# A one-layer NSA trunk: last output piece stored in two, a bias table written in longer runs, bias loads placed later

## The chip, the cores and the metric

One core of a Trainium2 chip runs the whole program. The metric is device time in microseconds of one execution. Shown are the median of three runs and one profiled execution, which the trace below belongs to.

## The reference, cut to what matters

One layer of native sparse attention on 512 tokens of width 1024, in float32, between two RMS norms:

```
u = rms_norm(x, pre_gain)
q, k/v (six sets), gates, z = u @ w_in
kc, vc = compress_kv(...)                 # a small two-layer net on blocks of 32 tokens
logits += table[t5_bucket(distance)]      # one bias table for all three branches
o = softmax branches (compressed, selected, window)
y = sum(gates * o * silu(z)) @ w_out
out = x + rms_norm(y, post_gain)
```

The bias depends only on the distance and the head. The kernel therefore makes two tables of it early on: `toepd`, 16 heads by 640 distances, for the window and selected branches, and `cmpb`, 1024 distances by 16 heads, for the compressed branch.

## The kernel before

All products run as three passes of split float32 (a high and a low part of each operand). Weights come in tiles of 512 KB (`load_raw`, L100, three buffers `wr`) and are split by `split_raw` (L106) into `wh` and `wl` (three buffers each): even tiles by ACT and POOL, odd ones by DVE alone (L240). SyncE (SP) issues nearly every transfer, in one queue, so an issue that waits holds up what is behind it. A scheduler lays out the order of each engine's instructions from the program text; the text's order is what the author controls.

**The head (0 to about 110 us).** `rms` and `prep` (L304, L311) make the normed, transposed input `uh`, `ul`. Then come the projection for compressed keys (`p_kc`, L367 to L377) and, between its two halves, `tables()` (L330). `tables()` multiplies a constant one-hot matrix by the bias table. For `cmpb` it does so in eight column blocks `j`: the 33x128 slice of `hcr` is loaded as weights and the 33x16 table `nth`, then `ntl`, streams through (L351, L352). The result, `cb`, has the distances on its 128 partitions, eight blocks of 16 heads each. Four stores (L356) bring it to DRAM, one for each group `g` of four heads:

```
for g in range(G):
    SP.dma_start(dview(cmpb, g * H * MC * R, [[R, 128], [128 * R, 8], [1, R]]), cb[:, g])
load_bias(0)
```

Partition `m` and block `j` hold distance `j*128 + m`, so each run in DRAM is R = 4 floats, 16 bytes, and a store has 1024 of them. `load_bias(0)` (L160) then loads four `bias` tiles from `toepd` (L163) and the compressed-branch bias `cbs` from `cmpb` (L168). `blocks` (L402) copies the projected keys, then values, out of PSUM in blocks (`blk`, L407, on DVE) and splits them (`bh` on ACT, L416; `bl` on DVE and POOL, L417). The loop at L472 projects `p_v` for both other value sets and runs the first layer of the compression net (`mlp`, L420); it reads tiles 4 to 11 of the weight order (tile 6 is the first one that SP asks for behind the bias loads).

**The tail.** `wout` (L820) multiplies by `w_out`, row tile by row tile in the order 0, 3, 2, 1. For the last one, each half of 512 columns is multiplied by the post gain into `g3` (L915); ACT sums its squares (L912); POOL makes the norm factor `ss` (`rstd`, L84). `finish` (L873) then does `xr = g3 * ss + xr` on DVE (L874) and stores the half from SP (L877):

```
for i in range(2):
    finish(*prev, i)
```

Of the kernel before, what the change touches and what calls it, by code (L numbers as in the profile page):

```python
# [14 lines left out]
ALU = mybir.AluOpType  # L15
# [4 lines left out]
S = 512  # L20
D = 1024
H = 16
DH = 64
G = 4
R = 4
# [9 lines left out]
MC = 64  # L35
# [11 lines left out]
def dview(ap, off, dims):  # L47
    return bass.AP(tensor=ap.tensor, offset=ap.offset + off, ap=dims)
# [3 lines left out]
def nsa_layer(ctx: ExitStack, tc: tile.TileContext, x, pre_gain, post_gain, table, w_in, w_out,  # L52
              k_pos, k_w1, k_w2, v_pos, v_w1, v_w2, hot, hot_c, out):
    nc = tc.nc
    V, A, P, T, SP = nc.vector, nc.scalar, nc.gpsimd, nc.tensor, nc.sync
    x = x.rearrange("b s d -> (b s) d")
    out = out.rearrange("b s d -> (b s) d")
# [102 lines left out]
    def load_bias(g):  # L160
        for hh in range(R):
            b = keep.tile([128, S], F32, name="bias", tag="bias", bufs=6)
            SP.dma_start(b, dview(toepd, (g * R + hh) * LT, [[1, 128], [1, S]]))  # L163
            bias[g * R + hh] = b
        c = keep.tile([128, NT, CP, R], F32, name="cbs", tag="cbs", bufs=1)
        for t in range(NT):
            src = dview(cmpb, (g * H * MC + 8 * t) * R, [[R, 8], [MC * R, 16], [1, CP * R]])
            SP.dma_start(c[:, t].rearrange("p c r -> p (c r)"), src)  # L168
        cbs[g] = c
# [90 lines left out]
    with tc.tile_pool(name="a1", bufs=1) as a1:  # L260
        grow = a1.tile([1, D], F32, name="grow")
        A.dma_start(grow, pre_gain)
        warm = a1.tile([1, 1], F32, name="warm")
        A.activation(warm, nhalf[0:1], AF.Tanh)
        one = a1.tile([1, 128], F32, name="one")
        V.memset(one, 1.0)
        ones = a1.tile([1, 128], F32R, name="ones")
        V.tensor_copy(ones, one)
        xs = []
        for t in range(NT):  # L270
            xt = a1.tile([128, D], F32, name="xt", bufs=4)
            SP.dma_start(xt, x[t * 128:(t + 1) * 128, :])
            xs.append(xt)
            if t == 1:
                load_ahead(1)
        tabx = a1.tile([33, H], F32, name="tabx")
        SP.dma_start(tabx[0:32], table)
        hots = a1.tile([33, LT], F32, name="hots")
        SP.dma_start(hots, hot)
        hotc = a1.tile([33, D], F32, name="hotc")  # L280
        SP.dma_start(hotc, hot_c)
        for nm, pos, w2 in (("k", k_pos, k_w2), ("v", v_pos, v_w2)):
            small[nm, "p"] = sm.tile([32, 2, DH], F32, name="pos" + nm)
            SP.dma_start(small[nm, "p"][:, 0], pos.rearrange("n l d -> (n l) d"))
            small[nm, "w"] = sm.tile([128, 2, DH], F32, name="w2" + nm)
            SP.dma_start(small[nm, "w"], w2.rearrange("n (k p) c -> p (n k) c", p=128))
        gain = []
        gh = a1.tile([1, D], F32R, name="gh")
        gl = a1.tile([1, D], F32R, name="gl")
        for i in range(2):  # L290
            hs = slice(i * 512, (i + 1) * 512)
            V.tensor_copy(gh[:, hs], grow[:, hs])
            V.tensor_tensor(gl[:, hs], grow[:, hs], gh[:, hs].bitcast(F32), op=ALU.subtract)
            p = sb()
            T.matmul(p, ones, gh[:, hs], start=True, stop=False)
            T.matmul(p, ones, gl[:, hs], start=False, stop=True)
            gain.append(p)
        sq = a1.tile([128, D], F32, name="sq")
        banks = [tb, ob, tb]
        nb_ = 0  # L300

        rs_ = {}

        def rms(t):  # L304
            ss = a1.tile([128, 1], F32, name="ss", bufs=4)
            tc.keep_in_program_order(A.activation(sq, xs[t], AF.Square, scale=1.0 / 32, accum_out=ss))
            r = a1.tile([128, 1], F32, name="r", bufs=4)
            rstd(r, ss)
            rs_[t] = r

        def prep(t):  # L311
            nonlocal nb_
            r = rs_[t]
            for kq in range(2):
                hs = slice(kq * 512, (kq + 1) * 512)
                V.scalar_tensor_tensor(xs[t][:, hs], xs[t][:, hs], r, gain[kq], op0=ALU.mult, op1=ALU.mult)
                p = banks[nb_ % 3]()
                nb_ += 1
                for j in range(4):
                    k = kq * 4 + j  # L320
                    T.transpose(p[:, j * 128:(j + 1) * 128], xs[t][:, k * 128:(k + 1) * 128], ident)
                for jj in range(2):
                    i = kq * 2 + jj
                    src = p[:, jj * 256:(jj + 1) * 256].rearrange("p (a b) -> p a b", a=2)
                    dh = uh[i][:, :, t * 128:(t + 1) * 128]
                    dl = ul[i][:, :, t * 128:(t + 1) * 128]
                    A.copy(dh, src)
                    V.tensor_tensor(dl, src, dh.bitcast(F32), op=ALU.subtract)

        def tables():  # L330
            ntab = a1.tile([33, H], F32, name="ntab")
            V.tensor_scalar(ntab[0:32], tabx[0:32], -1.0, None, op0=ALU.mult)
            V.memset(ntab[32:33], BIG)
            nth = a1.tile([33, H], F32R, name="nth")
            ntl = a1.tile([33, H], F32R, name="ntl")
            V.tensor_copy(nth, ntab)
            V.tensor_tensor(ntl, ntab, nth.bitcast(F32), op=ALU.subtract)
            hsr = a1.tile([33, LT], F32R, name="hsr")
            hcr = a1.tile([33, D], F32R, name="hcr")
            A.copy(hsr, hots)  # L340
            A.copy(hcr, hotc)
            for o, n in ((0, 512), (512, LT - 512)):
                p = sb()
                T.matmul(p[:H, :n], nth, hsr[:, o:o + n], start=True, stop=False)
                T.matmul(p[:H, :n], ntl, hsr[:, o:o + n], start=False, stop=True)
                V.tensor_copy(toep[:, o:o + n], p[:H, :n])
            SP.dma_start(toepd, toep)
            cb = sm.tile([128, G, 8, R], F32, name="cb")
            p = sb()
            for j in range(8):  # L350
                T.matmul(p[:, j * H:(j + 1) * H], hcr[:, j * 128:(j + 1) * 128], nth, start=True, stop=False)  # L351
                T.matmul(p[:, j * H:(j + 1) * H], hcr[:, j * 128:(j + 1) * 128], ntl, start=False, stop=True)  # L352
            V.tensor_copy(cb.rearrange("p g j r -> p j g r"),
                          p[:, :8 * H].rearrange("p (j g r) -> p j g r", g=G, r=R))
            for g in range(G):
                SP.dma_start(dview(cmpb, g * H * MC * R, [[R, 128], [128 * R, 8], [1, R]]), cb[:, g])  # L356
            load_bias(0)

        rms(0)
        rms(1)  # L360
        prep(0)
        split_ahead(0)
        prep(1)
        split_ahead(1)
        rms(2)
        rms(3)
        p_kc = [pj(), pj()]  # L367
        for hh in range(2):
            hs = slice(hh * 256, (hh + 1) * 256)
            for k in range(KT):  # L370
                if hh == 0 and k in (3, 5):
                    prep(2 if k == 3 else 3)
                h, l = tiles[k // 4]
                for m in range(2):
                    ms = slice(m * 128, m * 128 + 128)
                    pass3(p_kc[m][:, hs], h[:, k % 4, ms], l[:, k % 4, ms], uh[k // 2][:, k % 2, hs],
                          ul[k // 2][:, k % 2, hs], k == 0, k == KT - 1)  # L377
            if hh == 0:
                tables()

    with tc.tile_pool(name="a2", bufs=1) as a2:
# [90 lines left out]
        for kp in range(4):  # L472
            h, l = tile_(n)
            for kk in range(2):
                k = kp * 2 + kk
                a, b = (v.rearrange("p (k a) c -> p k (a c)", k=2)[:, kk] for v in (h, l))
                for t in range(NT):
                    ts = slice(t * 128, (t + 1) * 128)
                    sh, sl = uh[k // 2][:, k % 2, ts], ul[k // 2][:, k % 2, ts]
                    T.matmul(p_v[t], sh, a, start=k == 0, stop=False)  # L480
                    T.matmul(p_v[t], sl, a, start=False, stop=False)
                    T.matmul(p_v[t], sh, b, start=False, stop=k == KT - 1)
            mlp(n + 1, kp, p_mk, kb)
            n += 2
        hs = silu2(p_mk)
        for t in range(NT):
            src = p_v[t].rearrange("p (i g d) -> p i g d", i=2, g=G)
# [10 lines left out]
        p = tb()  # L498
# [321 lines left out]
    def wout():  # L820
# [49 lines left out]
        def last(i):  # L870
            return tc.keep_in_program_order(i)
# [8 lines left out]
        for j, t in enumerate(turn):  # L880
# [43 lines left out]
                    for i in range(2):  # L924
                        finish(*prev, i)
            prev = t, xr, ss
        for i in range(2):
            finish(*prev, i)

    def kproj(g0):  # L930
        alloc_kd(g0)
# [95 lines left out]
```

## Time and profile before

| | |
|---|---|
| median of three runs | 466.47 us (466.29 to 467.47) |
| the profiled execution's own time | 466.85 us |
| its span, first to last instruction | 465.0 us |
| mean granted TensorE clock | 0.993 |
| PE busy | 450.9 us, 97% of the span |
| DVE, ACT, POOL busy | 330.6, 274.3, 184.7 us |
| share of PE in the chain that ended last | 89% |

The profiled execution lies 0.38 us above the median of the runs, and its time is 1.85 us longer than its span. PE is TensorE's matrix work and PEld its weight loads; the idle time of the other engines matters only where PE waits for one of them.

### The profile page before, as it was taken

The page shows a single profiled execution, that of the slowest core. Times are in us where ns is not written, and L with a number is a line of the kernel's source. Part 1 is how long each engine was busy: PE and PEld are TensorE (multiplying, and loading weights), DVE is VectorE, ACT ScalarE, POOL GpSimd, SP SyncE. Part 2 cuts the span into 40 slices and gives each one's busy share as a digit, 9 for nine tenths or more (in the row PEclk, how much of TensorE's full clock was granted, in tenths as well). Part 3 has the DMA queues.
Part 4 walks back from the last instruction along what each step waited for, and adds up shares of the span by engine and source line. Part 5 has one row for each costly group of instructions (what it writes and reads, how often), then busy time and mean ns, then how long its engine had stood idle before and what let it go on. Part 6 is the DMA issues. An engine that isn't in the chain of part 4 may idle for free.

```text
span 465.0 us, 6924 instructions
## 1 busy us (share of the span) xinstructions
PE 450.9 (97%) x2330; PEld 375.3 (81%) x2330; DVE 330.6 (71%) x801; ACT 274.3 (59%) x642; POOL 184.7 (40%) x185
## 2 busy tenths in 40 slices
PE   5999999999999999999999999999999999999994
PEld 4797888878888878888888788888878888888883
DVE  6869844851766888768769776885896667567685
ACT  5712232542766577767846867666776666467541
POOL 4424544242223453342463525245343342448212
PEclk9989999999999999999999999999999999999998
DMA  8489275263111321511132332024051211214113
GB/s 300 142 82 280 77 216 162 66 206 90 47 45 48 112 59 34 182 45 47 45 90 70 88 94 71 21 57 132 19 180 45 92 45 47 91 43 140 47 45 135
DMA packets 45501, 44.63 MB, mean 96 GB/s; under 512 B 7751, under 2 KB 38471, under 8 KB 45466
## 3 DMA queue, kind: packets, MB, share of 16 engines
q1 hardware_dynamic: 44424, 44.00, 31.9%
q8 instruction: 18, 0.29, 0.3%
q10 hardware_dynamic: 1042, 0.20, 0.2%
q14 instruction: 17, 0.14, 0.1%
HBM read 41.99 MB, written 2.20 MB: 95 GB/s over the span
## 4 chain that ended last, share of the span: by engine, by line
PE 89%; DVE 4%; ACT 3%; issue 2%; POOL 1%; DVEq 0%; POOLq 0%; ACTq 0%
PE ps_pj L146 11%; PE ps_pj L148 11%; PE ps_pj L147 11%; PE ps_s L591 9%; PE ps_t L681 7%; PE ps_o L715 4%; PE ps_o L714 4%; PE ps_pj L834 3%; PE ps_pj L835 3%; PE ps_pj L836 3%; PE ps_s L247 2%; PE ps_s L248 2%; PE ps_s L249 2%; PE ps_pj L247 2%; PE ps_pj L248 1%
## 5 line engine op out<-in xcount | busy, mean ns | idle before, releaser
L118 POOL TENSOR_TENSOR wl<-wr,wh 128x512 fp32r<-128x512 f32 x94 | 123.0, 1328 | 138.6 <-ACT wh L113 122.2
L146 PE MATMUL ps_pj<-uh,wh 128*128 128x512 f32 x240 | 99.0, 412 | 0.0
L148 PE MATMUL ps_pj<-ul,wh 128*128 128x512 f32 x240 | 94.2, 393 | 0.0
L147 PE MATMUL ps_pj<-uh,wl 128*128 128x512 f32 x240 | 94.2, 392 | 0.0
L604 ACT ACTIVATE p<-p,nm 128x512 f32<-128x512 f32 (+3 forms) x128 | 71.6, 560 | 24.3 <-DVE nm L603 23.5
L685 DVE TENSOR_TENSOR ptl<-ps_t,pth 128x512 fp32r<-128x512 f32 x80 | 55.0, 688 | 28.2 <-ACT pth L684 27.7
L113 ACT CAST wh<-wr 128x1024 fp32r<-128x1024 f32 x47 | 49.2, 1047 | 43.5 <-DMA wr<-in_nsa_w_in_dram 20.1
L591 PE MATMUL ps_s<-kd,q 128*128 128x512 f32 (+5 forms) x256 | 63.9, 336 | 0.7 <-DVE zs L699 0.6
L684 ACT CAST pth<-ps_t 128x512 fp32r<-128x512 f32 x80 | 46.4, 580 | 29.3 <-PE ps_t L681 28.7
L148 PEld LDWEIGHTS ps_pj<-ul,wh 128*128 128x128 f32 x240 | 45.1, 188 | 10.1
L591 PEld LDWEIGHTS ps_s<-kd,q 128*128 128x128 f32 x256 | 43.9, 189 | 9.0 <-DVE zs L699 1.2
L146 PEld LDWEIGHTS ps_pj<-uh,wh 128*128 128x128 f32 x240 | 45.2, 188 | 6.1
L147 PEld LDWEIGHTS ps_pj<-uh,wl 128*128 128x128 f32 x240 | 45.3, 189 | 5.8
L603 DVE CUSTOM_DVE_ANT_0 p<-ps_s,bias 128x128 f32<-128x128 f32 (+3 forms) x80 | 34.6, 447 | 20.7 <-PE ps_s L591 20.5
L681 PE MATMUL ps_t<-ident,p 128*128 128x128 f32 x320 | 48.4, 272 | 0.0
L681 PEld LDWEIGHTS ps_t<-ident,p 128*128 128x128 f32 x320 | 39.7, 140 | 9.4
L714 PE MATMUL ps_o<-pth,vt 128*128 128x512 f32 x80 | 33.7, 421 | 0.0
L603 DVE CUSTOM_DVE_ANT_1 p<-ps_s,bias 128x256 f32<-128x256 f32 (+2 forms) x48 | 26.3, 555 | 9.3 <-PE ps_s L591 8.6
L728 POOL TENSOR_TENSOR y<-otmp,zs 128x256 f32<-128x256 f32 x16 | 12.3, 771 | 51.5 <-DVE otmp L725 51.5
L715 PE MATMUL ps_o<-ptl,vt 128*128 128x512 f32 x80 | 32.3, 404 | 0.0
L730 POOL TENSOR_TENSOR otmp<-otmp,zs 128x256 f32<-128x256 f32 x15 | 11.1, 741 | 37.9 <-DVE otmp L725 37.9
L569 ACT ACTIVATE zs<-ps_pj 128x512 f32<-128x512 f32 x22 | 13.1, 596 | 19.4 <-PE ps_pj L148 19.3
(268 smaller groups left out, 895.6 us busy)
## 6 DMA issues: line engine op xcount, KB each, us to landing
wr<-in_nsa_w_in_dram SPq DMA_DIRECT2D x36, 512.0 KB
wr<-in_nsa_w_in_dram SPq DMA_DIRECT2D x16, 256.0 KB
bias<-toepd SPq DMA_DIRECT2D x16, 256.0 KB
wr<-in_nsa_w_out_dram SPq DMA_DIRECT2D x8, 512.0 KB
xt<-in_x_dram SPq DMA_DIRECT2D x4, 512.0 KB
wr<-in_nsa_cmp_k_w_dram SPq DMA_DIRECT2D x4, 512.0 KB
wr<-in_nsa_cmp_v_w_dram SPq DMA_DIRECT2D x4, 512.0 KB
xr<-in_x_dram SPq DMA_DIRECT2D x8, 256.0 KB
```

Of the source, the lines that this page charges most:

```text
L113: A.copy(h[:, 0:kn], raw[:, 0:kn])
L118: el.tensor_tensor(l[:, ks], raw[:, ks], h[:, ks].bitcast(F32), op=ALU.subtract)
L146: T.matmul(p, a, rh, start=k == 0, stop=False)
L147: T.matmul(p, b, rh, start=False, stop=False)
L148: T.matmul(p, a, rl, start=False, stop=k == KT - 1)
L591: T.matmul(po, qs[h][:, qt * 128:(qt + 1) * 128], kds[h // R][:, i, c0:c0 + n], start=i == 0, stop=i == 1)
L603: V.tensor_tensor_reduce(pd, src, bi, 1.0, BIG, ALU.add, ALU.min, st["nm"][:, hh:hh + 1])
L604: A.activation(po, po, AF.Exp, bias=st["nm"][:, hh:hh + 1], scale=-1.0, accum_out=st["rs"][:, hh:hh + 1])
L681: T.transpose(tp[:, hh * 128:(hh + 1) * 128], st["p"][hh][:, c:c + 128], ident)
L685: V.tensor_tensor(pl, tp, ph.bitcast(F32), op=ALU.subtract)
L714: T.matmul(acc, v, ph, start=j == 0, stop=False)
L715: T.matmul(acc, v, pl, start=False, stop=j == qt)
```

## The change

Three edits. (1) In `tables()` the weights of block `j` are now the columns `j, j+8, j+16, ...` of `hcr` (a stride of eight floats, 32 bytes) instead of 128 neighbours. Partition `m` then holds the distances `8m` to `8m+7`, and a group's store writes one run of 8*R floats, 128 bytes, from each partition. (2) `load_bias(0)` is called after the loop at L472 and no longer inside `tables()`. (3) The last row tile's second half is finished in two pieces of 256 columns; the first is stored from ACT's queue, the second from SP's.

```diff
+            hcj = hcr.rearrange("p (m j) -> p j m", j=8)
             for j in range(8):
-                T.matmul(p[:, j * H:(j + 1) * H], hcr[:, j * 128:(j + 1) * 128], nth, start=True, stop=False)
-                T.matmul(p[:, j * H:(j + 1) * H], hcr[:, j * 128:(j + 1) * 128], ntl, start=False, stop=True)
+                T.matmul(p[:, j * H:(j + 1) * H], hcj[:, j], nth, start=True, stop=False)
+                T.matmul(p[:, j * H:(j + 1) * H], hcj[:, j], ntl, start=False, stop=True)
...
-                SP.dma_start(dview(cmpb, g * H * MC * R, [[R, 128], [128 * R, 8], [1, R]]), cb[:, g])
-            load_bias(0)
+                SP.dma_start(dview(cmpb, g * H * MC * R, [[8 * R, 128], [1, 8 * R]]),
+                             cb[:, g].rearrange("p j r -> p (j r)"))
...
             mlp(n + 1, kp, p_mk, kb)
             n += 2
+        load_bias(0)
         hs = silu2(p_mk)
...
-        for i in range(2):
-            finish(*prev, i)
+        t, xr, ss = prev
+        finish(t, xr, ss, 0)
+        for c, q_ in ((0, A), (256, SP)):
+            cs = slice(c, c + 256)
+            last(V.scalar_tensor_tensor(xr[1][:, cs], g3[1][:, cs], ss, xr[1][:, cs], op0=ALU.mult, op1=ALU.add))
+            q_.dma_start(out[t * 128:(t + 1) * 128, S + c:S + c + 256], xr[1][:, cs])
```

What the scheduler made of it: the queue of SP in the head, from the `toepd` store on (`wr` are weight tiles; line numbers of the changed kernel are a few higher).

```order
 L347 DMA toepd<-toep 16x640
-L356 DMA cmpb<-cb 128x8x4 x4
-L163 DMA bias<-toepd 128x512 x4
+L357 DMA cmpb<-cb 128x32 x4
+L163 DMA bias<-toepd 128x512
+L103 DMA wr<-in_nsa_w_in_dram 128x2x256 x2
+L163 DMA bias<-toepd 128x512
+L103 DMA wr<-in_nsa_cmp_k_w_dram 128x4x256
+L163 DMA bias<-toepd 128x512 x2
 L168 DMA cbs<-cmpb 128x1x128 x4
-L103 DMA wr<-in_nsa_w_in_dram 128x2x256 x2
-L103 DMA wr<-in_nsa_cmp_k_w_dram 128x4x256
```

The weight tiles 6 (two transfers of 128x2x256) and 7 moved ahead of three of the four bias loads and of the four `cbs` loads; one bias load still stands ahead of them.

The end of DVE's queue before:

```order
L915 TENSOR_TENSOR og_5065<-ps_pj,pgain 128x512
L874 SCALAR_TENSOR_TENSOR xr<-og_5032,fss,xr 128x512
L874 SCALAR_TENSOR_TENSOR xr<-og_5065,fss,xr 128x512
L1023 UNCONDITIONAL_BRANCH
```

and in the change:

```order
L917 TENSOR_TENSOR og_5065<-ps_pj,pgain 128x512
L876 SCALAR_TENSOR_TENSOR xr<-og_5032,fss,xr 128x512
L933 SCALAR_TENSOR_TENSOR xr<-og_5065,fss,xr 128x256 x2
L1029 UNCONDITIONAL_BRANCH
```

ACT's queue, which ended with the last sum of squares, now ends with the store of the first piece:

```order
L914 ACTIVATE junk,sumsq<-ps_pj 128x512
L934 DMA out_dram<-xr 128x256
L1029 UNCONDITIONAL_BRANCH
```

On all engines the order of everything else is the same in both kernels, line numbers aside.

## Rows read from the trace of the kernel before

**Rows 1.** What PE waited for from 20 to 95 us: total, times, longest.

```profile
PE ps_s L480 <- DVE blk L407: 0.6, 1, 0.6
PE ps_o L427 <- DVE wl L118: 0.4, 1, 0.4
```

**Rows 2.** Timeline of SP's queue in the head: start us, us until the last issue, transfer.

```profile
23.45 0.33 SPq L347 DMA_DIRECT2D toepd<-toep  x1
25.07 3.17 SPq L356 DMA_DIRECT2D cmpb<-cb  x4
28.34 2.50 SPq L163 DMA_DIRECT2D bias<-toepd  x4
30.88 5.54 SPq L168 DMA_DIRECT2D cbs<-cmpb  x4
37.63 1.03 SPq L103 DMA_DIRECT2D wr<-in_nsa_w_in_dram  x2
```

**Rows 3.** Timeline of ACT, POOL and DVE: tile 6 split, first readers of bias and `cbs`.

```profile
43.46 1.05 ACT L113 CAST wh<-wr 128x1024 fp32r<-128x1024 f32 x1 [4.65 <-DMA wr<-in_nsa_w_in_dram]
44.59 2.52 POOL L118 TENSOR_TENSOR wl<-wr,wh 128x512 fp32r<-128x512 f32 x2 [3.66 <-ACT wh L113]
...
116.20 0.69 DVE L603 CUSTOM_DVE_ANT_0 p<-ps_s,bias 128x512 f32<-128x512 f32 x1 [3.39 <-PE ps_s L591]
121.44 0.38 DVE L656 TENSOR_TENSOR lc<-ps_s,cbs 128x128 f32<-128x128 f32 x1 [0.47 <-PE ps_s L591]
```

**Rows 4.** Timeline of PE: last reader of tile 3, the wait, first reader of tile 6.

```profile
41.71 0.39 PE L249 MATMUL ps_s<-ul,wh 128*128 128x512 f32 x1
...
44.98 0.47 PE L480 MATMUL ps_s<-wh,uh 128*128 128x512 f32 x1 [0.61 <-DVE blk L407]
...
49.63 0.40 PE L480 MATMUL ps_pj<-wh,uh 128*128 128x512 f32 x1
```

**Rows 5.** Timeline of PE: first and last of the 16 small matmuls, and what follows.

```profile
22.77 0.27 PE L351 MATMUL ps_s<-nth,hcr 33*128 33x16 f32 x1
...
24.46 0.25 PE L352 MATMUL ps_s<-ntl,hcr 33*128 33x16 f32 x1
...
25.02 0.41 PE L248 MATMUL ps_pj<-uh,wl 128*128 128x256 f32 x1
...
27.80 0.41 PE L249 MATMUL ps_pj<-ul,wh 128*128 128x256 f32 x1
...
28.17 0.28 PE L248 MATMUL ps_pj<-uh,wl 128*128 128x256 f32 x1
...
30.44 0.28 PE L249 MATMUL ps_pj<-ul,wh 128*128 128x256 f32 x1
```

**Rows 6.** Busy us by stretch: PE, PEld, DVE, ACT, POOL, then PEclk, DMA share, GB/s.

```profile
24.60:28.00 3.40, 3.40 (x17) 3.38 (x17) 1.36 (x5) 0.00 (x0) 0.52 (x1) 0.51 0.91 136
```

**Rows 7.** Groups by shape, weight loads of 22 to 25 us: busy, mean ns.

```profile
L351 PEld LDWEIGHTS ps_s<-nth,hcr 33*128 33x128 f32 x8 | 1.5, 187 | 0.1
```

**Rows 8.** Groups by shape, DVE from 110 to 145 us: 128 columns, strided and not.

```profile
L603 DVE CUSTOM_DVE_ANT_0 p<-ps_s,bias 128x128 f32<-128x128 f32 x2 | 0.5, 284 | 0.0
...
L656 DVE TENSOR_TENSOR lc<-ps_s,cbs 128x128 f32<-128x128 f32 x1 | 0.4, 380 | 0.5 <-PE ps_s L591 0.5
```

**Rows 9.** Timeline of DVE: a split beside a busy POOL, and one beside an idle POOL.

```profile
38.09 1.73 DVE L417 TENSOR_TENSOR bl<-blk,bh 128x496 fp32r<-128x496 f32 x1
...
41.38 0.68 DVE L118 TENSOR_TENSOR wl<-wr,wh 128x512 fp32r<-128x512 f32 x1
```

**Rows 10.** Timeline of the end: DVE's last two instructions and SP's last two stores.

```profile
460.72 1.42 DVE L874 SCALAR_TENSOR_TENSOR xr<-og,fss,xr 128x512 f32<-128x512 f32 x2 [0.35 <-POOL fss L90]
461.50 0.33 SPq L877 DMA_DIRECT2D out_dram<-xr  x1
462.16 0.33 SPq L877 DMA_DIRECT2D out_dram<-xr  x1
```

**Rows 11.** Groups by shape, DVE from 440 to 466 us: 512 and 256 columns.

```profile
L907 DVE TENSOR_TENSOR og<-og,ps_pj 128x512 f32<-128x512 f32 x3 | 2.1, 688 | 1.2 <-PE ps_pj L836 1.2
...
L731 DVE TENSOR_TENSOR y<-y,otmp 128x256 f32<-128x256 f32 x1 | 0.4, 419 | 0.0
```

**Rows 12.** Stretches as in rows 6: the first bias and `cbs` transfers, the last stores.

```profile
30.00:36.00 6.00, 6.00 (x30) 4.94 (x30) 5.06 (x11) 1.05 (x1) 2.55 (x2) 1.00 0.88 34
...
462.30:463.70 1.40, 0.00 (x0) 0.00 (x0) 0.00 (x0) 0.00 (x0) 0.00 (x0) 0.50 0.98 369
```

## The prediction, made before the changed kernel ran

> **What bounds the kernel now.** The page comes first: PE is busy for 97% of the span and makes up 89% of the chain that ended last. An edit therefore pays only where PE waits, where PE itself works longer, or after PE's last matmul. Next, the list of what PE waited for, cut to the stretch that the edits touch (20 to 95 us). It holds two waits, 0.61 and about 0.4 us, and both are for DVE, none for a transfer [rows 1, 4]. Nothing that only moves transfers can win more than those 1.0 us. The timelines then tell who needs what and when, and the stretch view gives the clock and the load on the DMA engines.
>
> **Edit 1, stores and bias loads.** In the head SP needs 3.17 us to issue four small `cmpb` stores, then 2.50 us for the bias loads and 5.54 us for `cbs` [rows 2]. From 30 to 36 us the DMA engines are busy for 0.88 of the time and move only 34 GB/s [rows 12]. The 16-byte runs keep them busy without moving much. With 128-byte runs a store has 128 pieces instead of 1024, and I take an ordinary issue of about 0.33 us for each, as the `toepd` store has [rows 2], so SP is free some 1.8 us sooner. Who gains? The readers of these tables start at 116.20 and 121.44 us, some 80 us after the loads [rows 3]. So the term is zero, and it would stay zero if the loads came 20 us later.
>
> **Edit 2, the loads moved back.** The two transfers of tile 6 are issued at 37.63 us [rows 2], behind the table loads. In the changed order only one bias load stands ahead of them, so they go out about 7 us earlier. ACT did wait 4.65 us for this tile [rows 3], which looks like a gain. But the cast needs a `wh` buffer, and tile 6 takes the one that tile 3 leaves. PE reads tile 3 until 41.71 plus about 0.4 us [rows 4]. The cast can start at about 42.1 instead of 43.46, and POOL's split ends at about 45.7 instead of 47.1 [rows 3]. PE first wants the tile at 49.63 [rows 4], so it was ready 2.5 us ahead and will be 3.9 us ahead. The term is zero. What is late at that place is DVE, in the chain of `blk` copies that PE waits for, and no edit touches that. On SP's queue a bias load now stands behind the issue of tile 7, which waits for ACT and POOL; only bias and `cbs` queue there, with 80 us to spare. The bounds of both terms together: no gain beyond the two waits, -1.0 us; the loss is the contention rival below.
>
> **Edit 1, the strided weights.** This is the one part on PE's own path. Sixteen pairs of a weight load and a 16-column matmul run from 22.77 to 24.46 us, 15 steps of 0.113 us [rows 5]; 16 columns need no such step, where 256 take 0.119 us, so the weight load sets it (187 ns each, begun before the one ahead has ended) [rows 5, 7]. The change loads the same 128 columns, each 32 bytes from the next. No weight load of the trace reads with a stride. Lower bound: the same load without one, +0. Upper bound: DVE reading the `cbs` table with a step of four floats takes 380 ns for 128 columns, where an operation of the same size on neighbours takes 284 ns [rows 8], +0.096 us for 128 elements; times 16 that is +1.5 us, and +1.8 us if each step doubles. I take +0, because the nearest row is the load itself: its 187 ns at a step of 113 ns says that loads overlap, so a slower access to each element has time to hide, which DVE's one instruction at a time has not. It is the weakest step here.
>
> The clock belongs to this place. Right behind the sixteen small matmuls the granted clock falls to 0.51, the lower of its two levels (1.2 GHz), until 28.0 us [rows 6]. The 256-column matmuls there are 0.214 us apart (25.02 to 27.80, 13 steps) and afterwards 0.119 us (28.17 to 30.44, 19 steps) [rows 5], so this stretch costs about 15 times 0.095 = 1.4 us. With equal small matmuls it stays as it is: +0. If they take longer, PE does little for longer, and the stretch can only grow or be spent on cheap work.
>
> **Edit 3, the tail.** Two instructions of 256 columns cost 2 x 419 against 688 ns for one of 512 [rows 11], so DVE ends 0.15 us later. The last SP store is issued at about 462.3 instead of 462.16 [rows 10] and carries half as much; the ACT store goes out at about 461.9. But the DMA engines are busy for 0.98 of the time from 462.3 to 463.7, at 369 GB/s: both stores of 256 KB follow each other without a gap [rows 12]. Their start hangs on the first store (461.50, 0.8 us ahead of the first bytes [rows 10, 12]), which the change leaves alone. The same 512 KB from the same start end at the same time, as long as the last piece arrives before 463.7: 462.3 + 0.8 + half of 0.7 = 463.45, so it does. Term: +0; bounds -0.2 (half of the last store's 0.7 us less DVE's 0.15) and +0.2 us (DVE's 0.15 and shorter runs).
>
> **Sum.** 466.85 us for the profiled execution, plus 0 + 0 + 0 + 0. That execution lies 0.38 us above the median, so I forecast 466.5 us, no change. A measurement of this kernel can tell some 0.3%, 1.4 us, from no change. Own range of this case: 465.8 to 467.3.
>
> **Rivals.**
> *Strided weights load slower (slower).* If what DVE shows in rows 8 holds for the weight port as well, each of the 16 steps grows by 0.096 us or up to double, +1.5 to +1.8 us, all on PE, as nothing else feeds PE there. That makes 468.1 us; it passes 0.3% once a step exceeds 0.20 us. With the stretch of little work twice as long, the low clock may also last longer, up to once more 1.4 us, 469.5. For it: DVE's row, and that nothing hides PE's work there. Against: the overlap in rows 7. The Trainium skill, "SBUF — State Buffer", in the section "Door 1: The DMA port swizzle", says that SBUF is read in 16-byte lines and that each access to a new line pays a penalty, so that float32 may step by up to four elements for free. By that rule a step of eight floats pays for every element, which is this rival; DVE's row already pays at a step of four, so the trace agrees that there is a price, and no run here shows it for a weight load. Chance 0.33.
>
> *Tile 6 early meets DVE (a little slower).* If ACT's cast came before 41 us, POOL's split would run beside DVE's of 41.38, and such a pair costs DVE 1.73 instead of 0.68 us [rows 9]; the `blk` chain and PE's wait grow by 1.0 us: 467.5. Against it stands the buffer of tile 3 [rows 4]. Chance 0.05.
>
> *The relief pays after all (faster).* Both PE waits go (-1.0) and the tail gives its -0.2: 465.3 us. For it: 7 us of earlier weights. Against: both waits name DVE [rows 1], and DVE's order is unchanged. Passing 0.3% would need the low clock to stay away too. Chance 0.10.
>
> **How the numbers follow.** Forecast 0.52; rivals 0.33, 0.05, 0.10. Slower by over 0.3%: three quarters of the strided rival, where the step doubles or the clock joins in, 0.25, and 0.02 for the rest, 0.27. Faster by over 0.3%: half of the last rival, 0.05. Within: 0.68. The range reaches from the faster rival, 465.4, to the strided rival with part of the clock's price, 468.9.
>
> **What would show it.** In the changed profile: the sixteen small matmuls still 0.113 us apart (0.2 us if the strided rival is right); granted clock 0.5 behind them for as long as before; `cmpb` stores issued within 1.5 us; tile 6 issued near 30 us and cast at about 42 us; the same 0.61 us wait of PE for `blk`; the DMA engines again full from about 462.3 to 463.7 us. The prediction is wrong if PE's work from 22 to 31 us is over 1.4 us longer or shorter, or the stretch after DVE's last instruction changes by over 0.5 us.

## The result, and the profile after

The changed kernel takes 470.26 us, median of six runs (469.43 to 471.88); the kernel before took 467.37 us in six runs (466.29 to 468.33), three of which are the runs shown ahead. The ratio is 1.0076, with a 95% interval of 1.0054 to 1.0098: slower, by 2.9 us, and above both ranges that the prediction names (465.8 to 467.3 and 465.4 to 468.9). The ratios are not quotients of the medians and can differ from them a little. One execution among all that follow, of the pairs issued twice, took 505.4 us at a mean clock of 0.85; ratios and counts leave it out.

The profiled execution took 469.59 us, its span 467.8 us, at a mean granted clock of 0.993. What PE waits for from 20 to 95 us is what it waited for before [rows 1] (the list of waits of the changed kernel: us in total, times, longest):

```profile
PE ps_s L481 <- DVE blk L408: 0.6, 1, 0.6
PE ps_o L428 <- DVE wl L118: 0.4, 1, 0.4
```

So the loss is not a wait. PE's own timeline shows it (start, us, engine, line, operation; the sixteen small matmuls, then the key projection's second half):

```profile
23.44 0.40 PE L352 MATMUL ps_s<-nth,hcr 33*128 33x16 f32 x1
23.70 0.38 PE L353 MATMUL ps_s<-ntl,hcr 33*128 33x16 f32 x1
23.94 0.38 PE L352 MATMUL ps_s<-nth,hcr 33*128 33x16 f32 x1
...
27.03 0.38 PE L353 MATMUL ps_s<-ntl,hcr 33*128 33x16 f32 x1
27.33 0.39 PE L247 MATMUL ps_pj<-uh,wh 128*128 128x256 f32 x1
...
33.10 0.28 PE L249 MATMUL ps_pj<-ul,wh 128*128 128x256 f32 x1
```

From the first small matmul to the last it is 3.59 us where it was 1.69 [rows 5]: 15 steps of 0.239 us instead of 0.113, +1.90 us. The last matmul of the projection starts 2.66 us later than before [rows 5]; of the rest, 0.67 us were there ahead of the first changed instruction (23.44 against 22.77), which the edits do not touch. Without what lies ahead, from the first small matmul to the last matmul of the projection, it is 9.66 us now and was 7.67. Behind the small matmuls both profiles have a stretch of 3.4 us at the lower level of the clock (1.2 GHz); before, from 24.60 to 28.00 us [rows 6], now (busy us of PE, PEld, DVE, ACT, POOL, then PEclk, DMA share, GB/s):

```profile
28.00:31.40 3.40, 3.40 (x18) 3.40 (x17) 2.02 (x5) 0.51 (x1) 0.04 (x1) 0.50 0.46 87
```

The weight loads behind the steps, grouped by shape (count, busy us, mean ns), were 187 ns [rows 7]:

```profile
L353 PEld LDWEIGHTS ps_s<-ntl,hcr 33*128 33x128 f32 x8 | 2.7, 332 | 0.0
L352 PEld LDWEIGHTS ps_s<-nth,hcr 33*128 33x128 f32 x8 | 2.6, 329 | 0.1
```

SP's queue shows that the two other edits of the head do what they say. The `cmpb` stores take 1.83 us to issue instead of 3.17, and tile 6 goes out at 31.80 instead of 37.63 us [rows 2], although everything here is late:

```profile
27.76 1.83 SPq L357 DMA_DIRECT2D cmpb<-cb  x4
29.69 0.74 SPq L163 DMA_DIRECT2D bias<-toepd  x1
31.80 0.90 SPq L103 DMA_DIRECT2D wr<-in_nsa_w_in_dram  x2
...
38.56 2.55 SPq L168 DMA_DIRECT2D cbs<-cmpb  x4
```

ACT casts that tile at 44.78 us; less the 2.66 us by which PE is late here that is 42.1, where the prediction put it. It now waits for the buffer that PE reads, not for the transfer [rows 3]:

```profile
44.78 1.05 ACT L113 CAST wh<-wr 128x1024 fp32r<-128x1024 f32 x1 [3.31 <-PE ps_s L249]
```

In the tail DVE finishes the last half in two pieces, and both stores leave their queues within 0.4 us of each other (timelines of DVE, ACT's queue and SP's queue; below, the stretch in which the DMA engines carry them, columns as above):

```profile
463.97 0.87 DVE L933 SCALAR_TENSOR_TENSOR xr<-og,fss,xr 128x256 f32<-128x256 f32 x2
464.48 0.37 ACTq L934 DMA_DIRECT2D out_dram<-xr  x1
464.87 0.33 SPq L934 DMA_DIRECT2D out_dram<-xr  x1
```

```profile
465.00:466.40 1.40, 0.00 (x0) 0.00 (x0) 0.00 (x0) 0.00 (x0) 0.00 (x0) 0.50 0.98 348
```

Theory A: the strided weight loads are the whole loss, 1.9 us by their steps and about 1 us by the low clock behind them (not in these two profiles, which have 3.4 us of it each). Its rival, theory B: the moved loads or the split tail carry a part of it.

### The profile page after: what moved, and what is told of

It reads as the page before. It is cut to its first block, busy times and chain, and to the rows that moved or that the text cites. A ratio compares the mean times of both kernels' runs of the same rounds, so it can differ in the third digit from the quotient of the medians.

```text
span 467.8 us, 6925 instructions
## 1 busy us (share of the span) xinstructions
PE 454.1 (97%) x2330; PEld 378.8 (81%) x2330; DVE 330.5 (71%) x802; ACT 274.0 (59%) x642; POOL 184.4 (39%) x185
## 4 chain that ended last, share of the span: by engine, by line
PE 93%; DVE 2%; ACT 2%; DMA 1%; issue 1%; SPq 0%; POOL 0%; POOLq 0%; DVEq 0%; ACTq 0%
PE ps_pj L146 11%; PE ps_pj L148 11%; PE ps_pj L147 11%; PE ps_s L593 9%; PE ps_t L683 7%; PE ps_o L717 4%; PE ps_o L716 4%; PE ps_pj L836 3%; PE ps_pj L837 3%; PE ps_pj L838 3%; PE ps_s L247 2%; PE ps_pj L247 2%; PE ps_s L248 2%; PE ps_s L249 2%; PE ps_pj L248 2%; PE ps_pj L249 2%
```

## The experiments

### The change without the stride

```diff
-                T.matmul(p[:, j * H:(j + 1) * H], hcj[:, j], nth, start=True, stop=False)
+                T.matmul(p[:, j * H:(j + 1) * H], hcr[:, j * 128:(j + 1) * 128], nth, start=True, stop=False)
...
-    feeds["hot_c"] = _hot((16 * m + r - 527).reshape(-1))
+    feeds["hot_c"] = _hot((16 * m + r - 527).reshape(128, 8).T.reshape(-1))
```

The columns of the constant one-hot matrix are permuted, so that neighbours are loaded and the 128-byte stores stay. `ntl` likewise.

> All of the change but the strided weight loads: the constant one-hot matrix is handed over with its columns in the new order, so the sixteen weight loads read neighbours, and the 128-byte stores, the moved bias loads and the two-piece tail stay as in the changed kernel. Theory A (the stride is the loss): the sixteen steps are 0.113 us again, PE's stretch from the first small matmul to the end of the key projection is 2.0 us shorter than in the changed kernel, and the time is within 0.6 us of the kernel before (ratio 0.999 to 1.0015). Theory B (the moved loads or the tail carry a good part): the time stays 1.0 us or more above the kernel before.

Measured: 466.67 us, median of 12 runs, beside 467.16 us of 23 runs of the kernel before on the same chip; ratio 0.9999 (0.9981 to 1.0017). Steps and weight loads are those of the kernel before (PE and PEld of this kernel):

```profile
22.58 0.27 PE L351 MATMUL ps_s<-nth,hcr 33*128 33x16 f32 x1
...
23.05 0.25 PE L351 MATMUL ps_s<-nth,hcr 33*128 33x16 f32 x1
23.16 0.25 PE L352 MATMUL ps_s<-ntl,hcr 33*128 33x16 f32 x1
...
28.76 0.28 PE L249 MATMUL ps_pj<-ul,wh 128*128 128x256 f32 x1
```

```profile
L352 PEld LDWEIGHTS ps_s<-ntl,hcr 33*128 33x128 f32 x8 | 1.5, 188 | 0.0
```

From the first small matmul to the last of the projection it is 6.18 us, 3.5 us less than in the changed kernel where 2.0 were expected. The other 1.5 us is the low clock, which this execution did not have: the granted clock is 1.00 throughout the head. The same instructions took 7.67 us in the profile before, so one low stretch of 3.4 us costs 1.5 us here. Without the stride the change is free, and worth nothing.

### The table edit alone, and the tail alone

The first kernel is the one before with edit 1 (strided weights and 128-byte stores), `load_bias(0)` still in `tables()`; the second is the one before with edit 3.

> The table edit alone on the kernel before: strided weight loads and 128-byte stores; bias loads and tail as before. Theory A: the whole loss is here, steps of 0.238 us, 15 times 0.125 = +1.9 us in every execution and the rest of +2.9 us from a longer stretch at the lower clock in some of them, so +1.9 to +3.4 us. Theory B: at most +1.9 us, with the low clock as long as before, and the remaining 1.0 us is missing.

Measured: 469.95 us (469.50 to 470.64, 6 runs), ratio 1.0070 (1.0054 to 1.0086), with the changed kernel's 1.0076 inside that interval. In this profile the clock stayed low for longer than in the changed kernel's (us of PE busy, PEclk, DMA share, GB/s):

```profile
26.00:28.00 2.00, 2.00 (x10) 0.64 0.03 8
28.00:30.00 2.00, 2.00 (x11) 0.50 0.65 125
30.00:32.00 2.00, 2.00 (x11) 0.50 0.53 132
32.00:34.00 2.00, 2.00 (x14) 0.66 1.04 302
```

At two levels, 1.0 and 0.5, these means make 1.4 + 2 + 2 + 1.4 = 6.8 us at the lower one, twice as long as the 3.4 us of [rows 6]. PE's timeline in the same execution:

```profile
23.51 0.40 PE L352 MATMUL ps_s<-nth,hcr 33*128 33x16 f32 x1
...
26.62 0.38 PE L353 MATMUL ps_s<-ntl,hcr 33*128 33x16 f32 x1
26.86 0.38 PE L352 MATMUL ps_s<-nth,hcr 33*128 33x16 f32 x1
...
34.31 0.28 PE L249 MATMUL ps_pj<-ul,wh 128*128 128x256 f32 x1
```

From the first small matmul to the last of the projection it is 10.80 us, 1.1 more than the changed kernel's 9.66 with half as much low clock. The clock fell at about 26.6 us, yet the strided step there is 0.24 us as at the full clock.

> The two-piece tail alone on the kernel before. Theory A (engines of the DMA set the end): from the end of PE's last matmul to the end of the span 0.0 to 0.3 us longer than before (6.5 us), the time within 0.4 us of the kernel before. Theory B: the second queue at the end costs more, 0.7 us or over.

Measured: 466.80 us (465.16 to 468.10, 12 runs), ratio 0.9996 (0.9978 to 1.0014). From the start of PE's last matmul to the end of the span it is 6.7 us (458.98 to 465.7) where it was 6.5 (458.46 to 465.0), within theory A's 0.3. Theory B falls: the whole loss comes with the table edit, and of that only with the stride.

### What a stride costs, size by size

```diff
-                T.matmul(p[:, j * H:(j + 1) * H], hcr[:, j * 128:(j + 1) * 128], nth, start=True, stop=False)
-                T.matmul(p[:, j * H:(j + 1) * H], hcr[:, j * 128:(j + 1) * 128], ntl, start=False, stop=True)
+                hs_ = hcr[:, 0:128 * (j + 1):j + 1]
+                T.matmul(p[:, j * H:(j + 1) * H], hs_, nth, start=True, stop=False)
+                T.matmul(p[:, j * H:(j + 1) * H], hs_, ntl, start=False, stop=True)
```

Pair `j` loads its 128 columns with a step of j+1 floats, so one execution holds all steps from 1 to 8. The table entries are those of other columns here.

> The kernel before with another stride in each of the eight pairs of small matmuls: 1, 2, 3, 4, 5, 6, 7 and 8 floats between the columns of a weight load. The table for the compressed branch is thereby filled with values of other distances. Theory line (a price for every element that lies in another 16 bytes than the one ahead): steps of 0.113 us at strides 1 and 2, in between at 3, and a flat 0.23 to 0.24 us from 4 on. Rival (the price grows with the distance): 0.113 us at 1, rising evenly to 0.238 us at 8, near 0.17 us at 4. Rival (a threshold beyond 16 bytes): 0.113 us up to 4, and 0.238 us from 5 on.

The timeline of PE in this kernel (468.79 us, one run), first matmul of each pair, steps 1 to 8, and the one that follows:

```profile
23.51 0.27 PE L352 MATMUL ps_s<-nth,hcr 33*128 33x16 f32 x1
...
23.75 0.26 PE L352 MATMUL ps_s<-nth,hcr 33*128 33x16 f32 x1
...
23.99 0.32 PE L352 MATMUL ps_s<-nth,hcr 33*128 33x16 f32 x1
...
24.34 0.37 PE L352 MATMUL ps_s<-nth,hcr 33*128 33x16 f32 x1
...
24.80 0.36 PE L352 MATMUL ps_s<-nth,hcr 33*128 33x16 f32 x1
...
25.25 0.36 PE L352 MATMUL ps_s<-nth,hcr 33*128 33x16 f32 x1
...
25.69 0.37 PE L352 MATMUL ps_s<-nth,hcr 33*128 33x16 f32 x1
...
26.15 0.38 PE L352 MATMUL ps_s<-nth,hcr 33*128 33x16 f32 x1
26.39 0.38 PE L353 MATMUL ps_s<-ntl,hcr 33*128 33x16 f32 x1
```

A pair takes 0.24 us at a step of 1 and of 2, 0.35 at 3, 0.46, 0.45, 0.44 and 0.46 at 4 to 7, and its two matmuls start 0.24 apart at 8. The price rises between 2 and 4 floats and then stays, as the theory had it; an even rise would have given a step of 0.17 us at 4, and a threshold beyond 16 bytes 0.113 us. The Trainium skill, "SBUF — State Buffer", section "Door 1: The DMA port swizzle", has lines of 16 bytes with a penalty for each new line, which fits the flat part: from a step of four floats on, every element lies in a line of its own. It also lets float32 step by up to four elements for free; here a step of four costs the full price and one of three half of it, and DVE's row [rows 8] paid at a step of four too, so for these weight loads the measurement decides against that figure. Nor does each new line cost something here: at a step of two floats every second element lies in a new line, and the step is still 0.12 us.

### The length of the stretch of small matmuls

The stride also holds PE on small matmuls for twice as long. Is it this that brings the low clock? The kernel before with each pair issued twice stays there about as long without a stride:

```diff
-                T.matmul(p[:, j * H:(j + 1) * H], hcr[:, j * 128:(j + 1) * 128], nth, start=True, stop=False)
-                T.matmul(p[:, j * H:(j + 1) * H], hcr[:, j * 128:(j + 1) * 128], ntl, start=False, stop=True)
+                for rep in range(2):
+                    T.matmul(p[:, j * H:(j + 1) * H], hcr[:, j * 128:(j + 1) * 128], nth, start=True, stop=False)
+                    T.matmul(p[:, j * H:(j + 1) * H], hcr[:, j * 128:(j + 1) * 128], ntl, start=False, stop=True)
```

> The kernel before with each of the eight pairs of small matmuls issued twice, weights contiguous: 32 steps of about 0.113 us instead of 16, so the stretch of small matmuls lasts about as long (3.6 us) as the strided one of the changed kernel (3.8 us), without a stride anywhere. The table entries are computed twice, the second pair over the first. Theory A2 (what the stride costs beyond its 1.9 us is the clock: a longer stretch of small matmuls makes the low clock behind it come in nearly every execution): 1.8 us of steps, the low clock (0.41 us per 512-column matmul) behind the stretch in nearly every run, median 469.0 to 469.6, ratio 1.004 to 1.006, and hardly a run under 467.5. Theory B2 (the low clock comes by chance, with the same frequency as before, and the strided kernels met it for another reason): 1.8 us of steps alone, median 468.2 to 469, and still a group of runs at 467 to 467.8.

Measured: 470.47 us, median of five (470.22 to 470.61), beside 466.56 us of the kernel before (23 runs); ratio 1.0068 (1.0052 to 1.0085). All five have the low clock (means of 0.989 or 0.993), as theory A2 expected. The price is 3.9 us by the medians and 3.2 by the ratio, for 16 more steps of 0.113 us, 1.8 us. Most of the rest is the clock, which in this profile fell inside the stretch and came back at about 31.3 us:

```profile
24.50:31.30 6.80, 6.80 (x34) 6.78 (x34) 0.54 (x2) 0.00 (x0) 0.52 (x1) 0.51 0.42 71
```

At the lower level the small matmuls themselves are 0.213 us apart, where they were 0.113 (PE):

```profile
25.03 0.36 PE L352 MATMUL ps_s<-nth,hcr 33*128 33x16 f32 x1
25.24 0.36 PE L353 MATMUL ps_s<-ntl,hcr 33*128 33x16 f32 x1
```

From the first small matmul to the last of the projection it is 11.04 us (22.79 to 33.83) instead of 7.67, 3.4 more. Another 0.5 us is neither steps nor clock directly: PE's wait for `blk` has grown from 0.6 to 1.1 us.

```profile
PE ps_s L481 <- DVE blk L408: 1.1, 1, 1.1
```

So the median lies 0.9 us above theory A2's upper end. (The 0.41 us in the expectation is the length of a 256-column matmul's record at the lower level; those start 0.214 us apart [rows 5].)

### The small matmuls apart

The opposite: the changed kernel without a stride, and each pair laid behind one of the eight steps of the key projection's second half. The matmuls between the pairs have 256 columns, not the 512 of the expectation.

```diff
...
+                if hh == 1:
+                    tables_j(k)
             if hh == 0:
                 tables()
+        tables_end()
```

> The changed kernel with contiguous weight loads (columns of the one-hot matrix permuted), and each of the eight pairs of small matmuls laid behind one of the eight steps of the second half of the key projection, so that 512-column matmuls stand between the pairs. Theory A2 (a stretch of nothing but small matmuls is what lets the clock fall): no low clock behind them in most runs, median 465.2 to 466, the upper group of runs (467 to 468.3) thin or gone. Theory B2 (the low clock there has another cause, such as the waits around it, or chance): both groups of runs as in the kernel before, median 466.3 to 467.2.

Measured: 467.99 us (467.00 to 468.65, 12 runs), ratio 1.0021 (1.0006 to 1.0036): slower, against A2's time. The clock did as A2 said: all twelve executions have a mean of 0.996 or more, and the profile holds 1.00 throughout the head. But the mixing has a price of its own (PE of this kernel):

```profile
23.85 0.28 PE L249 MATMUL ps_pj<-ul,wh 128*128 128x256 f32 x1
24.06 0.27 PE L354 MATMUL ps_s<-nth,hcr 33*128 33x16 f32 x1
24.20 0.25 PE L355 MATMUL ps_s<-ntl,hcr 33*128 33x16 f32 x1
24.38 0.39 PE L247 MATMUL ps_pj<-uh,wh 128*128 128x256 f32 x1
24.60 0.29 PE L248 MATMUL ps_pj<-uh,wl 128*128 128x256 f32 x1
24.72 0.28 PE L249 MATMUL ps_pj<-ul,wh 128*128 128x256 f32 x1
```

One 256-column matmul follows another after 0.12 us, but it takes 0.21 us into a pair, 0.18 out of it and 0.22 behind the first matmul of 128 rows: a pair costs 24.60 - 23.85 - 2 x 0.12 = 0.51 us instead of 0.22. With seven more changes there and back than before that makes an estimated 7 x 0.29 = 2.0 us, against a saving in only some executions. PE's wait for `blk` also grew from 0.6 to 1.0 us.

### Beside 512-column matmuls, with the stride and without

The pairs stand between the 512-column matmuls of the value projection's first half; once with contiguous weights, once with the strided ones.

```diff
...
                 pass3(p, h[:, kk, ms], l[:, kk, ms], uh[k // 2][:, k % 2, :], ul[k // 2][:, k % 2, :],
                       k == 0, k == KT - 1)
+                if extra is not None:
+                    extra(kk * 2 + m)
...
+        half_t(2, 0, p_vc, tables_j)
```

> The changed kernel with contiguous weight loads, and the eight pairs of small matmuls moved behind the first 512-column matmuls of the first half of the value projection, with a bank of their own; the position tables and that half are brought forward to stand there. Theory A (nothing needs the table entries as early as they are computed, and PE is what bounds this stretch): the 1.8 us of small matmuls no longer stand as a quiet stretch, but each still takes its own time on PE, so the median is 465 to 466.5, with few runs in the upper group. If the entries are needed sooner than that, the wait of the first 0.6 us grows, or another stands at the reader of the table, and the time is 467 or more.

> As the run before it, but with the strided weight loads of the changed kernel (and its columns of the one-hot matrix in their own order). Theory A3 (a strided weight load of about 0.23 us runs beside the matmul ahead of it; beside a 512-column matmul of 0.23 us it is hidden, beside a small one it is not): of each pair, the load behind the 512-column matmul is hidden and that behind the small one is not, so the loss is half of the 1.9 us or less: 0.3 to 1.0 us above the contiguous one. Theory B3 (a strided load occupies PE and is hidden beside nothing): the whole 1.9 us, 467 to 468.5.

Measured: 468.14 us (12 runs), ratio 1.0025 (1.0011 to 1.0039), and 469.93 us (6 runs), ratio 1.0057 (1.0040 to 1.0074). The first misses theory A's 465 to 466.5. The reason seen in the spread kernel is there again: in its timeline a pair costs 29.57 - 28.59 - 2 x 0.23 = 0.52 us beside 512-column matmuls, while PE's wait for `blk` is shorter than before, 0.3 us. The second is 1.8 us above the first: theory A3 falls, B3's size of 1.9 us holds (not its 467 to 468.5, as the kernel beneath is slower than expected). The weight loads of the strided kernel tell why (PEld; in brackets its idle time before):

```profile
28.89 0.19 PEld L249 LDWEIGHTS ps_s<-ul,wh 128*128 128x128 f32 x1
29.44 0.31 PEld L358 LDWEIGHTS ps_o<-nth,hcr 33*128 33x128 f32 x1 [0.36 <-issue]
29.65 0.33 PEld L359 LDWEIGHTS ps_o<-ntl,hcr 33*128 33x128 f32 x1
30.00 0.19 PEld L247 LDWEIGHTS ps_s<-uh,wh 128*128 128x128 f32 x1
```

The first load of 33 rows begins at 29.44, the very start of its own matmul, and PEld was idle for 0.36 us before it, beside the 512-column matmul of 29.11. The same idle time stands there in the contiguous kernel (0.36 to 0.37 us). So nothing hid the load; the premise of A3 was not met. Whether a strided load of 128 rows would be hidden there was not tried. These eighteen executions also have mean clocks of 0.995 or more: 1.8 us is the price of the stride with the low clock out of play.

### Two halves instead of one

The kernel before with four pairs where all eight stood, and four behind the projection's second half, next to the 32-row transposes; in the second version the copy and the stores of the table come behind the `blk` sums in the program.

```diff
...
             if hh == 0:
                 tables()
+        tables_j(4)
+        tables_end()
```

> The kernel before (contiguous weight loads, its own table rows, bias loads and tail), with the eight pairs of small matmuls cut in two: four pairs where all eight stood, four behind the second half of the key projection, ahead of the 32-row transposes; the copy of the table entries and their four stores follow the second four. Theory A2 (the low clock follows a long enough stretch of small matmuls): each stretch is 0.9 us instead of 1.8, so the low clock comes in few runs or none and the median is that of the upper-clock runs of the kernel before and what one more change between 33-row and 128-row weights costs (0.28 us by the spread kernel), 465.3 to 466.3, ratio 0.996 to 0.999. If the vector engine's copy of the entries, now ahead of the position copies, shows as a longer wait at the first key projection of the next stage, 0.2 to 0.4 us are to be added. Theory B2 (the low clock comes by chance whatever the stretch): both groups of runs as in the kernel before and a median of 466.6 to 467.4.

> As the run before it, with the entries in a bank of their own, so that the vector engine copies them and SP stores them only behind the block sums of the next stage; the first four pairs then stand directly behind the matmuls of the Toeplitz rows. Theory A2: 465.1 to 466.0, the wait of the first 0.6 us as in the kernel before. Theory B2: 466.6 to 467.4, two groups of runs.

Measured: 467.34 us (465.97 to 468.43) and 466.84 us (465.71 to 468.27), 12 runs each, beside 467.13 us of 23 runs; ratios 0.9999 (0.9986 to 1.0013) and 0.9991 (0.9977 to 1.0006). Neither is told from the kernel before. Of these 24 executions 22 have no low clock in the head (means of 0.996 or more), so that half of A2 holds; the gain that was expected from it did not come. In both profiles PE waits 1.0 us for `blk` instead of 0.6 (the second version's list of waits):

```profile
PE ps_s L491 <- DVE blk L417: 1.0, 1, 1.0
```

DVE is later there: the scheduler now puts its split of `wgs` (0.55 us) between the first `blk` sums and the second, and these start 11.25 us apart instead of 10.95. In the first version PE also waits 0.5 us for `wl` at 57 us, where there was no wait before, in the second 0.2. The one more change of rows costs an estimated 0.3 us, by the spread kernel. How much each of these took is not shown apart. Beside the executions of the kernel before that had no low clock on this occasion (466.61 us), the first version's median is 0.7 us longer, and the ten of the second without low clock have the same 466.60.

### The low clock, counted

One low stretch of 3.4 us takes 3.4 x 0.5 / 465 = 0.004 off an execution's mean clock, so each execution's mean tells whether it had one. In all twelve profiles the granted clock is 1.00 from 40 us to the last matmuls at about 457 us; the lower level comes only in the head and behind them. Of 69 executions of the kernel before beside these kernels, 34 show 0.992 to 0.994 and 35 show 0.996 to 0.999, and the former are 1.0 to 1.8 us longer (medians 467.49 against 465.75 us, 468.06 against 466.27, 467.63 against 466.61 on the three occasions). All 17 of the changed kernel, the table edit alone and the pairs issued twice show 0.989 to 0.993. The kernel without the stride shows the low values in 5 of 12, the tail alone in 6 of 12, the five that lay the small matmuls apart in 2 of 54 (two more, at 0.995, lie between the groups).

## Why the prediction was wrong

The step that failed is the one under **Edit 1, the strided weights**: "I take +0, because the nearest row is the load itself: its 187 ns at a step of 113 ns says that loads overlap, so a slower access to each element has time to hide". Loads overlap about as much as before, and hide nothing: each began 0.07 us before the one ahead had ended (187 less 113 ns) and now begins 0.09 us before, and load (332 ns) and step (0.239 us) both grew by 0.13 to 0.14 us. In this chain of loads, which sets PE's pace, the overlap stayed and the whole growth of a load showed in the step. The term is +1.9 us, 0.1 us over the upper bound of +1.8 us. It also passes the prediction's own sign of being wrong: PE's work in the head is 2.0 us longer, over 1.4. DVE's row [rows 8], a strided read on another engine, was near (0.096 us a step against 0.126), the unstrided load on the same engine was not. That row compares two kinds of operation; by TENSOR_TENSOR rows on neighbours in the same list, 357 ns for 192 columns and 421 for 256, one of 128 would take an estimated 0.29 us, so the reading holds. That the two engines pay alike for one reason is not shown.

By the text's own words the rival *Strided weights load slower* came true, with its remark that the low clock "may also last longer". The frequency was what that remark missed: all 17 executions with the longer stretch of small matmuls have the low clock, where half had it before. The table edit alone is 2.8 us above the kernel before by the medians and 3.2 by the means (470.05 against 466.84). A reckoning from the timelines comes to 3.3: 1.9 us of steps, 1.5 us for a low stretch in the 10 of 23 executions that had none (0.65), and 1.1 us for a second one in the 4 of 6 whose mean clock is 0.990 or 0.991 (0.73). These two parts of the clock were not measured apart. That the length of the small-matmul stretch brings the low clock is shown by the pairs issued twice (no stride, five of five) and by the strided pairs laid apart (none of six); how the chip decides is not.

The other steps held, but for the base:

- **Edit 1, stores.** +0, held. Four stores take 1.83 us to issue, not the 1.5 us or less that the text looked for.
- **Edit 2.** +0, held, and by its mechanism: ACT's wait changed from the transfer to the buffer that PE reads, and the cast came at the 42.1 us of the forecast once PE's delay is taken off. The kernel without the stride keeps both PE waits at 0.6 and 0.4 us.
- **The clock with equal small matmuls** stays as it is: held (5 of 12 executions without the stride, against 13 of 23 beside them).
- **Edit 3.** +0, held: 0.9996 alone, an interval from -1.0 to +0.7 us, and 0.2 us by the trace, the upper bound; the DMA engines carry the last two stores at a share of 0.98, as before [rows 12].
- **The base** did not hold: the forecast started from a median of three runs, 466.47 us; with some executions at the low clock and some not, six runs gave 467.37. That moves the base by 0.9 us, not the ratio. The text took the low stretch for a fixed part of the kernel, at 1.4 us; its price was right (1.5 by the timelines), its coming each time was not.

## What to carry to other kernels

Price a strided operand by a row in which something reads with such a stride, even on another engine, rather than by the unstrided form of the same instruction: here the one gave +1.5 us, the other 0, and +1.9 was measured. Put the stride where nothing waits for it, here into the constant, which gave the same 128-byte stores at no cost. Where small matmuls set PE's pace, count them as time at PE's full price and look at the clock behind them: making that stretch longer cost more than its own steps. Breaking it up is not free either: each pair laid apart among 128-row weights took 0.3 us more.

## What the runs showed of the hardware that was not expected

- Weight loads of 128 float32 columns: steps of 0.11 to 0.12 us at an element step of 1 and 2, 0.17 at 3, 0.22 to 0.24 at 4 to 8.
- The lower clock level lengthened the contiguous step from 0.113 to 0.213 us and that of 256-column matmuls from 0.119 to 0.214, but not the strided one: 0.24 us at either level, in the few steps at the lower one that a trace has.
- A weight load of 33 rows did not begin beside the running matmul of 128 rows ahead of it (PEld idle 0.36 us, with the stride and without), while among themselves the loads of 33 rows do begin early, by 0.07 us without the stride.
- The lower clock level came in lengths of 3.4 us and of 6.8 us in the profiles read, and in the kernel before in half of the executions (34 of 69) with the same instructions.
